# Attention pieces of the second half at doubled distances among the matrix products

## The chip, the cores and the metric

The kernel runs on one core of one Trainium2 chip. A core has five engines with queues of their own: TensorE (matrix products, written PE; its weight loads are written PEld), VectorE (DVE), ScalarE (ACT), GpSimd (POOL) and SyncE (SP), which here only issues transfers. Matrix products read SBUF and write PSUM, the accumulator memory; the weights come from HBM by DMA. The metric is the device time of one execution in microseconds. Three runs of the kernel before gave 2150.22, 2152.0 and 2154.43; the median is 2152.0.

## What is computed

A decoder trunk of two layers on 256 tokens of width 2048, all in float32. Cut to what matters:

```python
for l in range(2):
    h = rmsnorm(x)
    q, k, v, gate_b, gate_c, conv_in = split(h @ w_in[l])   # six parts of 1024 columns
    # 8 heads; each has two score maps m = 0, 1 of width 64
    s = einsum('bqhmd,bkhmd->bhmqk', q, k) * scale + bias   # causal
    p = softmax(s)
    p = p[:, :, 0] - lam * p[:, :, 1]                       # differential attention
    attn = rmsnorm(einsum('bhqk,bkhd->bqhd', p, v)) * (1 - lam_init)
    conv = gate_b * short_conv(gate_c * conv_in)            # 3 taps, causal
    x = x + concat([attn, conv]) @ w_out[l]
    x = x + square(relu(rmsnorm(x) @ w_up[l])) @ w_down[l]
```

## The kernel before, in words

Each layer is a *mixer* (attention and convolution, up to w_out) followed by an *mlp*. TensorE is meant to run matrix products without a break, and everything else is threaded between them. Every float32 product is made of three products of split operands: a weight tile `raw` is loaded by SP (L343), ACT copies its rounded high part to `whi` (L302), DVE subtracts to get the low part `wlo` (L303). `Weights.take` hands out such a pair and has the next three prepared. There are four `raw` buffers and three pairs, so the loads, ACT and DVE follow TensorE at a fixed distance.

The mixer makes its products in this order: q, k, v for heads 0 to 3; q, k, v for heads 4 to 7; then for each of four quarters of the convolution gc (gate_C) and ci (conv_in); then gb (gate_B) four times; then the output projection o. The gc, ci and gb products are made by `linear_t` (products at L408): each takes four weight tiles, and for each tile it issues eight products 512 wide with `whi` and eight 256 wide with `wlo`. After every four of these it calls `work.tick()`. One such tick is a *step*; a weight tile is four steps, a gc or ci product sixteen.

`work` is a list of background pieces, written as generators. `yield n` hands back and asks to go on n steps later; what is issued between two yields stands at that place in TensorE's program. TensorE's order is this order of tracing, kept as it is; the order on DVE, ACT, POOL and SP is chosen by a scheduler that simulates the times, so it follows from where the pieces are traced.

`attention(..., pace)` is such a piece, called once for heads 0 to 3 with pace 1 and once for heads 4 to 7 with pace 2. The second call begins 9 steps into the products gc. Each head is a generator `unit(i)` of three parts:

1. score: eight products into two PSUM banks (`sc`, L604); DVE adds the bias and takes the row maximum (L610), ACT the exponentials (L619), DVE the reciprocal sums and the difference of the two maps, into `s` (L622 to L630).
2. transpose: three transposes of `s` into a bank (`ptp`, L635); ACT and DVE make the high and low parts `pT` (L637, L638).
3. value: six products `av` (L646, L648); ACT and DVE add their parts into `ao` (L651, L652), and ACT sums the squares (L654).

The last head goes on with the norm: five small operations on POOL (L661 to L664), two multiplications `an` on DVE (L668), and, after a further distance, the transposes `atp` (L677) from which ACT and DVE write the output projection's operand `cat` (L681, L682). `staggered` starts the four heads a fixed number of steps apart and passes one step at a time.

Buffers that matter: three PSUM banks for `sc`, `ptp`, `atp` in turn, one bank for `av`, two buffers of `s`, one of `pT`, one of `ao`. The mlp's pool for the up weights (`uraw`, four buffers of 1 MB, loaded by SP at L809) lies in SBUF where the attention's bias, `s`, `pT` and `ao` were. So the first four loads of `uraw` can go out only when the attention is done with these; they stand in SP's queue among the loads of `raw`.

Of the kernel before, what the change touches and what calls it, by code (L numbers as in the profile page):

```python
# [88 lines left out]
def staggered(pieces, apart):  # L89

    entries = [[i * apart, p] for i, p in enumerate(pieces)]
    while entries:
        for e in list(entries):
            if e[0] <= 0:
                try:
                    e[0] = max(1, next(e[1]))
                except StopIteration:
                    entries.remove(e)
                    continue
            e[0] -= 1  # L100
        if entries:
            yield 1
# [3 lines left out]
def trunk(ctx: ExitStack, tc: tile.TileContext, x, w_in, w_out, conv_w, q_norm_g, k_norm_g,  # L106
# [19 lines left out]
    def bank(name):  # L126
        return ps.tile([P, CH], F32, tag="bank", name=name)
# [456 lines left out]
    def attention(l, qT, kT, kL, v, h0, dst, bias, tmp, pace):  # L584
# [9 lines left out]
        def unit(i):  # L594
# [31 lines left out]
            for t in range(NT):  # L626
# [2 lines left out]
                                               nlam[:, l:l + 1], op0=ALU.mult, op1=ALU.mult)  # L629
                nc.vector.scalar_tensor_tensor(p[:, w], s[:, 1, w], c[:, t:t + 1], s[:, 0, w],  # L630
                                               op0=ALU.mult, op1=ALU.add)
            yield 10
            tp = bank(f"ptp{h}")
            for b in range(3):
                nc.tensor.transpose(tp[:, b * P:(b + 1) * P], p[:, b * P:(b + 1) * P], ident)  # L635
            pT = tmp.tile([P, 2, 3 * P], F32R, tag="pT", name=f"pT{h}", bufs=1)
            nc.scalar.activation(pT[:, 0], tp[:, :3 * P], AF.Copy)  # L637
            nc.vector.tensor_sub(pT[:, 1], tp[:, :3 * P], pT[:, 0].bitcast(F32))  # L638
            yield 4

            av = ps.tile([P, CH], F32, tag="av", name=f"av{h}", bufs=1)
            av = av.rearrange("p (t n c) -> p t n c", t=NT, n=2)
# [23 lines left out]
            for t in range(NT):  # L666
# [3 lines left out]
                    ao[:, t].rearrange("p (g d) -> p g d", d=P),  # L670
                    f2[:, :, t:t + 1].to_broadcast([P, 4, P]), op=ALU.mult)
                an_.append(an)
            yield 12 if pace == 1 else 18
            for t in range(NT):
                tp = bank(f"atp{h0}_{t}")
                for b in range(4):
# [7 lines left out]
                    op0=ALU.mult, op1=ALU.subtract)  # L684
                yield 2

        yield from staggered([unit(i) for i in range(4)], 8)
        dst.ready = True

    def conv(l, q, u, cv, norm):  # L690
# [25 lines left out]
    def mixer(l, norm, loads):  # L716

        with ExitStack() as scope:
# [28 lines left out]
            for half in range(2):  # L747
                h0 = 4 * half
                acc = linear(f"q{l}{half}", hT, weights)
                r = norm.r  # L750
                qT = bpool.tile([P, 2, 4, S], F32R, tag="b", name=f"qT{l}{half}")
                work.start(qk_norm(acc, r, q_parts(qT), q_gain[:, l:l + 1], f"q{l}{half}"))
                acc = linear(f"k{l}{half}", hT, weights)
                kT = bpool.tile([P, 2, 4, S], F32R, tag="b", name=f"kT{l}{half}")
                work.start(qk_norm(acc, r, k_parts(kT, kL), k_gain[:, l:l + 1], f"k{l}{half}"))
                acc = linear(f"v{l}{half}", hT, weights)
                v = bpool.tile([P, 2, NT, CH], F32R, tag="b", name=f"v{l}{half}")
                for t in range(NT):
                    nc.scalar.activation(v[:, 0, t], acc[:, t], AF.Copy, scale=r[:, t:t + 1])
                    nc.vector.scalar_tensor_tensor(v[:, 1, t], acc[:, t], r[:, t:t + 1],  # L760
                                                   v[:, 0, t].bitcast(F32),
                                                   op0=ALU.mult, op1=ALU.subtract)
                work.start(attention(l, qT, kT, kL, v, h0, cat[half], bias, tmp,
                                     1 + half), 3 + 6 * half)
# [477 lines left out]
```

## Time and profile before

| what | value |
|---|---|
| median of three runs | 2152.0 |
| profiled execution | 2151.32 |
| span of its trace | 2149.5 |
| granted TensorE clock | 1.000 |
| PE busy | 2134.0 (99%) |
| PEld busy | 1819.9 (85%) |
| DVE busy | 1678.6 (78%) |
| ACT busy | 1308.2 (61%) |
| POOL busy | 169.8 (8%) |
| HBM traffic over the span | 221 GB/s |

The span is the time from the first to the last instruction; the profiled execution's own time is 1.8 longer. Busy times are sums over instructions. Matmuls are pipelined: one begins before the one ahead of it has ended, so lengths in a list of matmuls overlap, and what a piece costs is read from the distance between starts. A line of the timeline gives start, length, engine, source line, operation, output and inputs, tile and count; a bracket gives the idle time ahead of it and the instruction whose end released it. "whi" and "wlo" are the halves of a weight tile, "raw" is the tile as loaded.

### The profile page before, as it was taken

The numbers are of one execution on the slowest core, as the hardware profiler recorded it, in microseconds if no ns is written. First come the engines' busy times: TensorE is split into PE (matmuls) and PEld (weight loads), VectorE is DVE, ScalarE is ACT, GpSimd is POOL, SyncE is SP. The second block draws the span as 40 slices with busy tenths as digits, with TensorE's granted clock in tenths as the row PEclk, the third lists the DMA queues.
The fourth block names the chain that finished last, engine by engine and source line by source line (L and its number), as shares of the span: only waits on it lengthen the run. The fifth ranks groups of instructions, "written<-read, shape, count | busy, mean of one in ns | idle before, by whom it ended". The sixth has DMA issues, their size and how long they took to land. (4 is left out here: it accounts for less than half of the span.)

```text
span 2149.5 us, 28983 instructions
## 1 busy us (share of the span) xinstructions
PE 2134.0 (99%) x10934; PEld 1819.9 (85%) x10934; DVE 1678.6 (78%) x2297; ACT 1308.2 (61%) x1767; POOL 169.8 (8%) x226
## 2 busy tenths in 40 slices
PE   9999999999999999999999999999999999999999
PEld 8888888888888888888888888888888888888887
DVE  6777655799889888798566776557888888888984
ACT  6666445666666666565566654446666666665652
POOL 3111100000000000011110111000000000001110
PEclk9999999999999999999999999999999999999999
DMA  8555766577777777798665566656777777777984
GB/s 271 179 160 171 246 186 187 190 244 230 233 232 231 229 227 234 241 318 288 210 178 176 166 197 215 187 176 204 241 233 223 240 229 226 235 225 262 335 264 137
DMA packets 298524, 475.98 MB, mean 221 GB/s; under 512 B 10803, under 2 KB 191621, under 8 KB 298384
## 3 DMA queue, kind: packets, MB, share of 16 engines
q1 hardware_dynamic: 268768, 406.88, 60.4%
q0 software_dynamic: 29568, 67.24, 9.4%
q8 instruction: 85, 1.39, 0.3%
q14 instruction: 55, 0.45, 0.1%
q10 hardware_dynamic: 48, 0.02, 0.0%
HBM read 440.52 MB, written 33.58 MB: 221 GB/s over the span
## 5 line engine op out<-in xcount | busy, mean ns | idle before, releaser
L303 DVE TENSOR_TENSOR wlo<-raw,whi 128x1024 fp32r<-128x1024 f32 x286 | 352.2, 1234 | 252.3 <-ACT whi L302 245.8
L302 ACT ACTIVATE whi<-raw 128x1024 fp32r<-128x1024 f32 x286 | 303.1, 1060 | 341.1 <-PE o L386 73.6
L949 PE MATMUL upc<-nT,uhi 128*128 128x512 f32 x1920 | 477.7, 391 | 0.6 <-ACT ev L959 0.6
L816 ACT ACTIVATE uhi<-uraw 128x1024 fp32r<-128x1024 f32 x256 | 271.2, 1060 | 280.3 <-PE upc L949 260.4
L949 PEld LDWEIGHTS upc<-nT,uhi 128*128 128x128 f32 x1920 | 352.7, 188 | 69.2 <-ACT ev L959 1.1
L817 DVE TENSOR_TENSOR ulo<-uraw,uhi 128x1024 fp32r<-128x1024 f32 x256 | 312.9, 1223 | 109.3 <-ACT uhi L816 105.3
L949 PEld LDWEIGHTS upc<-nT,ulo 128*128 128x128 f32 x1920 | 261.9, 190 | 18.7
L949 PE MATMUL upc<-nT,ulo 128*128 128x256 f32 x1920 | 267.7, 282 | 0.0
L386 PE MATMUL o<-whi,cat 128*128 128x512 f32 x512 | 159.5, 390 | 0.0
L1074 PE MATMUL dn<-whi,fb 128*128 128x512 f32 x480 | 151.1, 389 | 0.0
L386 PEld LDWEIGHTS o<-whi,cat 128*128 128x128 f32 x512 | 96.1, 188 | 19.7
L302 ACT ACTIVATE whi<-uraw 128x1024 fp32r<-128x1024 f32 x60 | 63.7, 1061 | 75.7 <-PE dn L1074 70.7
L1074 PEld LDWEIGHTS dn<-whi,fb 128*128 128x128 f32 x480 | 90.1, 188 | 18.7
L386 PE MATMUL o<-wlo,cat 128*128 128x512 f32 x256 | 99.6, 389 | 0.0
L840 DVE TENSOR_TENSOR t13l<-t,t13h 128x1024 fp32r<-128x1024 f32 x78 | 95.5, 1224 | 4.0 <-ACT t13h L839 2.2
L839 ACT ACTIVATE b2h<-draw 128x1024 fp32r<-128x1024 f32 x78 | 82.5, 1058 | 24.9 <-PE pr L992 22.2
L840 DVE TENSOR_TENSOR b2l<-draw,b2h 128x1024 fp32r<-128x1024 f32 x78 | 95.5, 1224 | 2.1 <-ACT b2h L839 2.1
L840 DVE TENSOR_TENSOR t24l<-t,t24h 128x1024 fp32r<-128x1024 f32 x78 | 95.2, 1221 | 1.4 <-ACT t24h L839 0.3
L853 DVE TENSOR_TENSOR t<-draw 128x1024 f32<-128x1024 f32 x78 | 95.3, 1221 | 0.4
L992 PE MATMUL pr<-t13h,f 128*128 128x512 f32 x240 | 93.8, 391 | 0.0
L1074 PE MATMUL dn<-wlo,fb 128*128 128x512 f32 x240 | 93.4, 389 | 0.0
L303 DVE TENSOR_TENSOR wlo<-uraw,whi 128x1024 fp32r<-128x1024 f32 x60 | 73.2, 1224 | 21.1 <-ACT whi L302 20.9
(408 smaller groups left out, 4138.6 us busy)
## 6 DMA issues: line engine op xcount, KB each, us to landing
uraw<-in_w_up_dram SPq DMA_DIRECT2D x128, 1024.0 KB, 6.5
raw<-in_w_in_dram SPq DMA_DIRECT2D x191, 512.0 KB, 4.0
draw<-in_w_down_dram SPq DMA_DIRECT2D x82, 1024.0 KB, 5.3
raw<-in_w_out_dram SPq DMA_DIRECT2D x64, 512.0 KB, 3.6
uraw<-in_w_down_dram SPq DMA_DIRECT2D x30, 1024.0 KB, 6.3
raw<-in_w_down_dram SPq DMA_DIRECT2D x16, 1024.0 KB, 5.2
hid0p<-f POOLq DMA_DIRECT2D x21, 512.0 KB, 6.4
fb<-hid0p POOLq DMA_DIRECT2D x21, 512.0 KB, 5.9
```

What stands on the lines that cost most here:

```text
L302: pair = (nc.scalar.activation(hi, raw, AF.Copy), nc.vector.tensor_sub(lo, raw, hi.bitcast(F32)))
L303: nc.vector.tensor_sub(lo, raw, hi.bitcast(F32)))
L386: nc.tensor.matmul(acc[:, t], a.ap[:, pa, k % KG, t * P:(t + 1) * P], (hi, lo)[pw][:, j], start=(k == 0 and n == 0), stop=(k == nk - 1 and ...
L816: pair = (nc.scalar.activation(hi, src, AF.Copy), nc.vector.tensor_sub(lo, src, hi.bitcast(F32)))
L817: nc.vector.tensor_sub(lo, src, hi.bitcast(F32)))
L839: keep(nc.scalar.activation(hi, src, AF.Copy))
L840: keep(nc.vector.tensor_sub(lo, src, hi.bitcast(F32)))
L853: keep(nc.vector.tensor_sub(t[:, 0:2], raw[:, :, 1], raw[:, 0]))
L949: nc.tensor.matmul(acc[:, 0] if part else acc, wt[:, k], a.ap[:, 0, k % KG] if part else a.ap[:, :, k % KG], start=(part == 0 and kh == 0 ...
L992: nc.tensor.matmul(prods[n], f[:, pa, a], b[pw], start=(start and m == 0), stop=(stop and m == 2))
L1074: nc.tensor.matmul(prods[p], f[:, pa, 2 * k + t], b[pw][:, n], start=(p in starts and k == 0 and m == 0), stop=(stop and k == 1 and m == 2))
```

## The change

In the attention all distances are multiplied by `pace`. For heads 0 to 3 pace is 1 and nothing changes. For heads 4 to 7 pace is 2: score to transpose is 20 steps in place of 10, transpose to value 8 in place of 4, `an` to `atp` 24 in place of 18, and the heads start 16 steps apart in place of 8. The number of instructions on each engine is the same.

```diff
-            yield 10
+            yield 10 * pace
             tp = bank(f"ptp{h}")
...
-            yield 4
+            yield 4 * pace

             av = ps.tile([P, CH], F32, tag="av", name=f"av{h}", bufs=1)
...
-            yield 12 if pace == 1 else 18
+            yield 12 * pace
             for t in range(NT):
                 tp = bank(f"atp{h0}_{t}")
...
-        yield from staggered([unit(i) for i in range(4)], 8)
+        yield from staggered([unit(i) for i in range(4)], 8 * pace)
```

Where this puts the pieces (a product's tiles counted from 0):

| piece | before | after |
|---|---|---|
| score, heads 4 / 5 / 6 / 7 | gc0 tile 2 / ci0 tile 0 / ci0 tile 2 / gc1 tile 0 | gc0 tile 2 / ci0 tile 2 / gc1 tile 2 / ci1 tile 2 |
| transpose, heads 4 / 5 / 6 / 7 | ci0 tile 0 / ci0 tile 2 / gc1 tile 0 / gc1 tile 2 | ci0 tile 3 / gc1 tile 3 / ci1 tile 3 / gc2 tile 3 |
| value, heads 4 / 5 / 6 / 7 | ci0 tile 1 / ci0 tile 3 / gc1 tile 1 / gc1 tile 3 | gc1 tile 1 / ci1 tile 1 / gc2 tile 1 / ci2 tile 1 |
| `atp` | gc2 tile 0 | gc3 tile 3 |

Before, the transposes and values stand between a tile's narrow products; after, between its wide ones. In SP's queue the first loads of `uraw` stand behind 20 of the mixer's gc and ci weight loads before; after, three stand behind 30 of them and the fourth behind 31. On POOL the five operations of the norm stand behind the gc and cv multiplications (L769, L700) of the first quarter before; after, also behind both of the second quarter and the gc one of the third. In ACT's order before, the `pT` copy of a head stands ahead of the next head's exponentials; after, it stands behind them.

## The prediction

> **What bounds the kernel now.** I read the page's busy times first, then the stretch in which the change acts, then TensorE's waits there, then the order of TensorE's work at each wait. All times are microseconds.
>
> The page's first lines:
>
> ```profile
> span 2149.5 us, 28983 instructions
> PE 2134.0 (99%) x10934; PEld 1819.9 (85%) x10934; DVE 1678.6 (78%) x2297; ACT 1308.2 (61%) x1767; POOL 169.8 (8%) x226
> ```
>
> TensorE is busy for all but 15.5 of the span. So a change that neither adds nor removes matmuls can move the time only by how long TensorE stands, or by how well neighbouring matmuls overlap.
>
> The second half of the attention (heads 4 to 7) runs among the products gc, ci of the convolution. The busy times of each engine in the stretch from the first gc product to the first gb product, layer 0 and then layer 1 (columns: length, PE, PEld, DVE, ACT, POOL, granted clock, DMA share, GB/s):
>
> ```profile
> 156.18:259.05 102.87, 100.52 (x597) 88.26 (x596) 70.87 (x132) 59.39 (x112) 15.43 (x12) 1.00 0.64 205
> 1222.63:1326.82 104.19, 100.55 (x598) 88.27 (x597) 70.86 (x132) 59.39 (x112) 15.43 (x12) 1.00 0.64 202
> ```
>
> DVE is busy 69% of it and ACT 58%, the clock is 1.00: neither is the bound over the stretch, they are late only in places. The waits of TensorE between 155 and 260 (engine, line, who was waited for: total, times, longest):
>
> ```profile
> PE ptp L635 <- DVE s L630: 0.8, 1, 0.8
> PE sc L604 <- DVE cat L682: 0.6, 1, 0.6
> PE av L648 <- DVE pT L638: 0.5, 1, 0.5
> PE ci L408 <- ACT whi L302: 0.3, 1, 0.3
> ```
>
> Two of these are waits of a head on itself: the transposes ptp on the probabilities s, the products av on the low half of pT. The idle times understate them, because a matmul that restarts has lost its overlap with the one before; so I price each from start to start against the same work on time. First a product tile without pieces, then TensorE's order of layer 0 around the pieces (columns: start, length, line, operation, count; the bracket is idle time and who ended it):
>
> ```profile
> 250.67 2.00 PE L408 MATMUL ci<-nT,whi 128*128 128x512 f32 x8
> 252.51 1.11 PE L408 MATMUL ci<-nT,wlo 128*128 128x256 f32 x8
> 253.46 2.00 PE L408 MATMUL ci<-nT,whi 128*128 128x512 f32 x8
> ...
> 158.95 1.09 PE L408 MATMUL gc<-nT,whi 128*128 128x512 f32 x4
> 161.24 0.64 PE L408 MATMUL gc<-nT,wlo 128*128 128x256 f32 x4
> 162.63 1.09 PE L408 MATMUL gc<-nT,whi 128*128 128x512 f32 x4
> ...
> 172.72 0.64 PE L408 MATMUL ci<-nT,wlo 128*128 128x256 f32 x4
> 173.19 0.49 PE L635 MATMUL ptp<-ident,s 128*128 128x128 f32 x3
> 173.44 0.72 PE L408 MATMUL ci<-nT,wlo 128*128 128x256 f32 x4
> ...
> 175.84 0.64 PE L408 MATMUL ci<-nT,wlo 128*128 128x256 f32 x4
> 176.96 0.69 PE L408 MATMUL ci<-nT,wlo 128*128 128x256 f32 x4
> ...
> 183.37 0.63 PE L408 MATMUL ci<-nT,wlo 128*128 128x256 f32 x4
> 184.63 0.33 PE L648 MATMUL av<-v,pT 128*128 128x128 f32 x1 [0.51 <-DVE pT L638]
> 185.26 0.69 PE L408 MATMUL ci<-nT,wlo 128*128 128x256 f32 x4
> 186.71 0.39 PE L604 MATMUL sc<-kT,qT 128*128 128x128 f32 x2
> 188.54 0.64 PE L408 MATMUL gc<-nT,wlo 128*128 128x256 f32 x4
> 189.50 0.72 PE L408 MATMUL gc<-nT,wlo 128*128 128x256 f32 x4
> 191.90 0.64 PE L408 MATMUL gc<-nT,wlo 128*128 128x256 f32 x4
> 193.24 0.69 PE L408 MATMUL gc<-nT,wlo 128*128 128x256 f32 x4
> 195.61 0.63 PE L408 MATMUL gc<-nT,wlo 128*128 128x256 f32 x4
> 197.09 0.83 PE L635 MATMUL ptp<-ident,s 128*128 128x128 f32 x3 [0.85 <-DVE s L630]
> 197.68 0.71 PE L408 MATMUL gc<-nT,wlo 128*128 128x256 f32 x4
> ```
>
> A tile of products takes 253.46 − 250.67 = 2.79: 1.84 for the eight wide ones, 0.95 for the eight narrow ones. It is four steps, so a step is 0.70. A ptp on time makes half a tile's narrow products last 0.72 (172.72 to 173.44), an av 1.12 (175.84 to 176.96). Against these, layer 0 loses:
> - last ptp, 195.61 to 197.68: 2.07 − 0.72 = 1.35
> - the ptp before it, 188.54 to 189.50: 0.96 − 0.72 = 0.24
> - av at 183.37 to 185.26: 1.89 − 1.12 = 0.77
> - av at 191.90 to 193.24: 1.34 − 1.12 = 0.22
>
> That is 2.58. The fourth wait comes later, after the attention; here it is in both layers, with the transfer that makes it late:
>
> ```profile
> 223.98 1.11 PE L408 MATMUL gc<-nT,wlo 128*128 128x256 f32 x8
> 225.42 2.11 PE L408 MATMUL ci<-nT,whi 128*128 128x512 f32 x8 [0.33 <-ACT whi L302]
> ...
> 1290.46 1.11 PE L408 MATMUL gc<-nT,wlo 128*128 128x256 f32 x8
> 1293.18 2.12 PE L408 MATMUL ci<-nT,whi 128*128 128x512 f32 x8 [1.62 <-ACT whi L302]
> ```
>
> ```profile
> 207.54 6.60 SPq L809 DMA_DIRECT2D uraw<-in_w_up_dram  x4
> ```
>
> ```profile
> 224.31 1.06 ACT L302 ACTIVATE whi<-raw 128x1024 fp32r<-128x1024 f32 x1 [6.50 <-DMA raw<-in_w_in_dram]
> 225.66 1.06 ACT L302 ACTIVATE whi<-raw 128x1024 fp32r<-128x1024 f32 x1 [0.29 <-DMA raw<-in_w_in_dram]
> ```
>
> When the attention's buffers fall free, SP issues four loads of 1 MB for the next stage (uraw), and the 0.5 MB weight loads behind them arrive late: ACT stood 6.50 on one. TensorE lost 225.42 − 223.98 − 0.95 = 0.49 in layer 0, and 1293.18 − 1290.46 − 0.95 = 1.77 in layer 1. The two stretches above differ by 1.32, which is this wait's 1.28 and nothing else: so layer 1 has the same 2.58 of head waits.
>
> **The change part by part.** No instruction is added or removed on any engine; the compiled orders differ only in this stretch of each layer.
>
> Score to ptp goes from 10 to 20 steps: 14.0 and the pieces between. The slowest chain shown is head 7's, 186.71 to 197.09 = 10.4. The ptp waits (1.35 + 0.24 a layer) go, with at least 3.6 to spare. ptp to av goes from 4 to 8 steps, 5.6; the worst av was late by 0.77 at half that, so 2.0 to spare. The av waits (0.77 + 0.22) go. Heads stand 16 instead of 8 steps apart, so one head's chain no longer runs into the next one's.
>
> Where a piece stands: ptp and av move from between narrow products to between wide ones. Four transposes between wide ones cost 161.24 − 158.95 − 1.84 = 0.45, between narrow ones 162.63 − 161.24 − 0.95 = 0.44. So 0.01 a piece, up to 0.02, for 16 pieces over both layers: I take 0.2 as a cost. The ends are 0.2 of gain and 0.6 of loss.
>
> The first sc of head 4 keeps its place and its 0.6 wait on the buffer that the first half's cat frees. Nothing is counted.
>
> SP: the uraw loads move from behind 20 of the turned loads of weights (gc, ci) to behind 30 (three of them), then one weight load, then the fourth. The first weight load after the burst has 3 MB ahead of it, not 4. Late loads drain one 0.5 MB tile per 1.35 (224.31 to 225.66, both as soon as they landed), so 1 MB is 2.7. In place of 0.49 and 1.77 late it comes 2.2 and 0.9 early. The next one still has 4 MB ahead and lands 1.35 after the time of the present first, but is needed a tile, 2.79, later: 0.49 − 1.44 and 1.77 − 1.44, so early in layer 0 and 0.3 late in layer 1. Of the 2.26 of this wait I take 1.96 as gone; the ends are 0 (the burst costs the same again) and 2.26. The uraw loads themselves start ten tiles later, some 28; they are covered by the gb products and the whole output projection that follow; without that cover the first up products would be late by as much as the shift.
>
> POOL: the five small operations of the heads' norm move behind three more multiplications (gc twice, cv once); an, atp and the second cat come later. atp has 24 steps, 16.8, behind the last av in place of 18, and cat is read only by the output projection, after all gb products. No cost; if that cover went, the output projection would wait at its second act.
>
> DVE and ACT do the same work. In the new order ACT has the four exponentials of head 5 ahead of head 4's pT, and so on: a new coupling, priced below as the slower rival.
>
> Sum: 2 × 2.58 + 1.96 − 0.2 = 6.9 less. The profiled execution took 2151.3 (span 2149.5 and 1.8 around it), so 2144.4; the median of the runs is 0.7 above the profiled one, so **2145.1**.
>
> The Trainium skill, "DMA: Bandwidth & Descriptors", section "Queues, rings and completion order", says that each DMA engine takes the descriptors of one ring in ring order, which is what the step from 4 MB to 3 MB rests on; the landing of the late tiles one after another, 1.35 apart, agrees. Its section "Issuing engines are not separate DMA queues" says that transfers in flight interleave on the same 16 engines; if that held within SP's one queue too, the fourth load, issued right behind the weight load, would take back part of what it gave, and the time would be that of the second rival.
>
> **The rivals.**
> - All head waits go, the burst costs what it cost (0.49 and 1.77, only later, among the ci and gb products). For it: 4 MB still go out in one go, with the same need of weights beside them. Against: one weight load now goes ahead of the fourth. Gain 5.16 − 0.2 = 5.0: 2147.0.
> - The waits only change their place. For it: with TensorE no longer held up by ptp and av, the weights must come faster, and whi, wlo share ACT and DVE with the heads. Against: DVE at 69% and ACT at 58% of the stretch, with the heads' work now thinner. Gain 0 to 2: 2151.
> - Slower. ACT takes instructions in order, so head 4's pT stands behind head 5's exponentials, head 5's behind head 6's, head 6's behind head 7's; three av pieces a layer hang on it. The slowest exponentials in the trace ended 194.73 + 0.19 − 186.71 = 8.2 after that head's sc:
>
> ```profile
> 194.73 0.19 ACT L619 ACTIVATION_READ_ACCUMULATOR s<-s,nm 128x1 f32 x1
> ...
> L637 ACT ACTIVATE pT<-ptp x16: 467/472/492, 101.9 to 1264.5; 128x384 fp32r<-128x384 f32 x16
> L638 DVE TENSOR_TENSOR pT<-ptp,pT x16: 547/551/556, 102.6 to 1266.1; 128x384 fp32r<-128x384 f32 x16
> ```
>
>   With 0.47 and 0.55 for the two halves of pT that is 9.2; av of the head before stands 12 steps behind that sc, 8.4, and the pieces between (sc itself, a ptp). So it is about on time even at the slowest chain shown, which ran among three heads at once. It turns the sign if each of the six av pieces waits 1.2 (6.9 / 6), that is, if the chain takes over 10.5. At 2 each the time is 2145.1 + 12 = 2157.
>
> **How the numbers follow.** Forecast 0.62, same burst 0.14, waits moved 0.12, slower 0.12. Run to run the times spread from 2150.22 to 2154.43, so about 0.2%, 4.3, is what can be told from no change: the border is 2147.7. The first two cases lie under it (0.76, of which I give 0.01 to the middle), the third in it: faster 0.75, same 0.13, slower 0.12. The forecast's own range is 2143 to 2147: 7.4 gone without any cost, or 5, and 1 for the medians. The asked range goes up to the third case and leaves the slower one out: 2142.8 to 2151.
>
> **What the profile after would show.** TensorE's waits without ptp on s and without av on pT; sc on cat still at 0.6, twice. The stretch from the first gc to the first gb product 102.87 − 3.07 + 0.1 = 99.9 in layer 0 and 104.19 − 4.35 + 0.4 = 100.2 in layer 1, nothing else moved. The uraw loads behind the second of the four loads of the last ci product, and ci or gb waiting on whi there by 0.3 at most. The forecast is wrong if av waits on pT in several heads (the slower rival), if ci or gb waits on whi by over 1 in both layers (the burst), or if wlo, whi waits turn up between pieces (waits moved).

## The result, and the profile after

The changed kernel takes 2144.35 (median of five runs, 2142.89 to 2145.03); the ratio to the kernel before is 0.9963, with a 95% interval of 0.9952 to 0.9974. The profiled execution took 2144.35 as well, 6.97 less than the profiled execution before. The page of the kernel after begins:

```profile
span 2142.6 us, 28965 instructions
PE 2131.4 (99%) x10934; PEld 1818.4 (85%) x10934; DVE 1684.2 (79%) x2297; ACT 1308.7 (61%) x1767; POOL 165.4 (8%) x226
```

All waits of TensorE over the whole span after (engine, line, who was waited for: total, times, longest):

```profile
PE pr L992 <- DVE f L982: 3.2, 2, 1.7
PE sc L604 <- DVE cat L682: 1.2, 2, 0.6
PE warm L160 <- DVE mhalf L152: 1.1, 1, 1.1
PE upc L949 <- ACT ev L959: 0.5, 1, 0.5
PE ci L408 <- ACT whi L302: 0.4, 1, 0.4
```

ptp and av are gone from the list, in both layers. sc has kept its 0.6, and of the wait of ci on whi 0.4 is left. The busy times from the first gc to the first gb product after, layer 0 and layer 1 (the first number behind the stretch is its length):

```profile
155.66:255.45 99.79, 99.18 (x597) 87.80 (x596) 73.63 (x132) 59.43 (x113) 13.20 (x12) 1.00 0.64 204
1220.05:1320.50 100.45, 99.45 (x598) 87.86 (x597) 73.17 (x132) 58.75 (x111) 13.20 (x12) 1.00 0.64 200
```

The stretches are 3.08 and 3.74 shorter, 6.82 together: the whole gain but 0.15 lies where the change was made.

The last head's transpose and what is left of the load burst, in TensorE's order after (start, length; the bracket is the idle time and who ended it):

```profile
217.21 1.09 PE L408 MATMUL gc<-nT,whi 128*128 128x512 f32 x4
218.14 0.49 PE L635 MATMUL ptp<-ident,s 128*128 128x128 f32 x3
218.39 1.17 PE L408 MATMUL gc<-nT,whi 128*128 128x512 f32 x4
...
1316.10 1.11 PE L408 MATMUL ci<-nT,wlo 128*128 128x256 f32 x8
1317.60 2.11 PE L408 MATMUL ci<-nT,whi 128*128 128x512 f32 x8 [0.39 <-ACT whi L302]
```

The transposes follow 0.93 behind the four wide products and take 0.25, with no gap. ci waits only in layer 1, 1317.60 − 1316.10 − 0.95 = 0.55.

The burst of `uraw` loads, SP's issues and ACT's copies behind it, in layer 0 and layer 1 after:

```profile
232.51 3.84 SPq L809 DMA_DIRECT2D uraw<-in_w_up_dram  x3
236.44 3.21 SPq L343 DMA_DIRECT2D raw<-in_w_in_dram  x1
239.70 1.23 SPq L809 DMA_DIRECT2D uraw<-in_w_up_dram  x1
...
1296.91 3.83 SPq L809 DMA_DIRECT2D uraw<-in_w_up_dram  x3
```

```profile
246.47 1.06 ACT L302 ACTIVATE whi<-raw 128x1024 fp32r<-128x1024 f32 x1 [1.30 <-DMA raw<-in_w_in_dram]
250.61 1.06 ACT L302 ACTIVATE whi<-raw 128x1024 fp32r<-128x1024 f32 x1 [3.08 <-DMA raw<-in_w_in_dram]
...
1312.41 1.06 ACT L302 ACTIVATE whi<-raw 128x1024 fp32r<-128x1024 f32 x1 [2.84 <-DMA raw<-in_w_in_dram]
1316.49 1.06 ACT L302 ACTIVATE whi<-raw 128x1024 fp32r<-128x1024 f32 x1 [3.02 <-DMA raw<-in_w_in_dram]
```

In layer 0 the first weight tile behind three loads is used 246.47 − 232.51 = 14.0 after the burst began; before, behind four loads, it was 224.31 − 207.54 = 16.8. The second is used at 18.1, that is about 16.8 and one tile of 1.35. Over all the kernels below these times spread; the last section has them.

### The profile page after: what moved, and what is told of

Same layout as the page of the kernel before. It is cut to its first block, busy times and chain, and to the rows that moved or that the text cites. A ratio compares the mean times of both kernels' runs of the same rounds, so it can differ in the third digit from the quotient of the medians.

```text
span 2142.6 us, 28965 instructions
## 1 busy us (share of the span) xinstructions
PE 2131.4 (99%) x10934; PEld 1818.4 (85%) x10934; DVE 1684.2 (79%) x2297; ACT 1308.7 (61%) x1767; POOL 165.4 (8%) x226
## 4 chain that ended last, share of the span: by engine, by line
PE 96%; DMA 1%; DVE 1%; ACT 1%; issue 0%; SPq 0%; DVEq 0%; ACTq 0%
PE upc L949 30%; PE pr L992 13%; PE o L386 8%; PE dn L1074 8%; PE gb L408 4%; PE k L386 4%; PE v L386 4%; PE ci L408 4%; PE q L386 4%; PE gc L408 3%; PE dn L1143 3%; PE dn L992 2%; PE pr1r L992 1%; PE pr0r L992 1%; PE upw L949 1%; PE up L949 1%
## 5 line engine op out<-in xcount | busy, mean ns | idle before, releaser
L303 DVE TENSOR_TENSOR wlo<-raw,whi 128x1024 fp32r<-128x1024 f32 x286 | 356.9, 1249 | 235.3 <-ACT whi L302 233.8
```

Source lines behind the costliest of these rows:

```text
L303: nc.vector.tensor_sub(lo, raw, hi.bitcast(F32)))
```

## The experiments

The theory that the runs were to test is narrower than the prediction, which let the doubled distances and the wider spacing work together: the head waits come from *crowding*, heads whose chains run into each other on DVE and ACT, so the spacing between the heads pays. The rival is *distance*: a head's own 10 and 4 steps are too short. The load burst is a second cause of its own.

The kernel before was run again beside the experiments, and each ratio is to these runs: its median was 2151.3 beside the runs with the spacing alone, three loads, transpose to value at 4 steps and the changed kernel two steps later, and 2153.06 beside the other four. The intervals of most of the faster kernels overlap, so they are told apart by their waits and not by their times.

**The spacing alone**

```diff
-        yield from staggered([unit(i) for i in range(4)], 8)
+        yield from staggered([unit(i) for i in range(4)], 8 * pace)
```

> Heads 4 to 7 start 16 steps apart as after the change, but the distances inside a head are the old ones (10, 4, 18). Theory (crowding): the waits of ptp and av come from heads running into each other on DVE and ACT, not from the distances inside a head, since head 4, which has no head before it, was on time with 10 and 4 steps. Then all the 5.2 us of head waits go here too, the load burst costs what it costs after the change (0 to 0.5), and the time is 2144 to 2146. Rival (distance): 10 steps, some 7 us and the pieces, are too short for the chain of a head that took up to 10.4 us; the ptp and av waits stay, only the burst's 2 us go, and the time is 2149 to 2151.

Measured: 2146.1 (2144.26 to 2147.42), ratio 0.9973 [0.9963, 0.9983]. TensorE's waits in this kernel, those of the attention and the products:

```profile
PE gc L408 <- ACT whi L302: 2.3, 3, 1.1
PE sc L604 <- DVE cat L682: 1.2, 2, 0.6
```

No ptp and no av wait is left, with 10 and 4 steps inside a head. That is crowding. A head's chain, from its first sc to the end of the last operation on s (L630), shows it directly: for head 7 of layer 0 it ran from 186.71 to 197.43 before, 10.7, and takes 6.2 here. The last line of the chain before, then both ends of it here:

```profile
196.69 0.74 DVE L630 SCALAR_TENSOR_TENSOR s<-s,c 128x128 f32<-128x128 f32 x2
...
203.21 0.39 PE L604 MATMUL sc<-kT,qT 128*128 128x128 f32 x2
208.69 0.74 DVE L630 SCALAR_TENSOR_TENSOR s<-s,c 128x128 f32<-128x128 f32 x2
```

The time lies 0.1 above the theory's range, since the burst cost more than I gave it: gc waits on whi for 2.3 in three places, 1.06 in layer 0:

```profile
242.66 2.14 PE L408 MATMUL gc<-nT,whi 128*128 128x512 f32 x8 [1.06 <-ACT whi L302]
```

The attention ends earlier here, and the burst goes out at another place relative to the tiles. The two stretches from first gc to first gb take 101.09 and 101.52, together 2.37 longer than in the changed kernel, which is about this wait. So of the 6.82 that the change takes from them, the spacing alone takes 4.45.

**The distances alone**

```diff
-            yield 10
+            yield 10 if pace == 1 else 14
...
-            yield 4
+            yield 4 * pace
```

> The other part alone: heads 8 steps apart as before the change, but score to transpose 14 in place of 10 and transpose to value 8 in place of 4. Theory (crowding): longer distances without more room between the heads only make more heads live at once. With two buffers of s, head 6's first work on DVE must wait until head 4's value is squared, behind step 22, while its score stands at step 16; its two banks stay taken, and head 7's score at step 24 waits on them for 1 to 3 us in each layer. The waits of ptp and av go or shrink, that of sc comes: 2149 to 2156. Rival (distance): the ptp and av waits go as in the changed kernel and nothing comes: 2145 to 2148.

Measured: 2153.2 (2151.22 to 2155.47), ratio 1.0003 [0.9994, 1.0011]: no gain at all. Its waits:

```profile
PE ptp L635 <- DVE s L630: 3.1, 2, 1.6
PE sc L604 <- DVE mx L610: 1.9, 2, 1.0
PE sc L604 <- DVE pT L638: 1.9, 2, 1.0
PE sc L604 <- DVE cat L682: 1.2, 2, 0.6
```

av is gone, as expected, and sc waits on its banks twice a layer instead. The ptp wait did not shrink, it grew from 0.8 to 1.6 each. It is head 7's, and the trace lays it to the buffer of s: head 7's first sc is at 185.86, but DVE takes its maxima only at 195.63, after ACT has squared head 5's values and so given its buffer back:

```profile
194.44 0.30 ACT L654 ACTIVATE s<-ao 128x128 f32<-128x128 f32 x1
...
195.63 0.27 DVE L610 CUSTOM_DVE_ANT_0 s<-sc,bias 128x128 f32<-128x128 f32 x1
```

The chains of heads 6 and 7 take 15.4 and 15.5 here: a longer distance makes a head hold its buffer longer. The burst's wait was smaller (0.6 in all, in layer 1). So these longer distances alone change one wait for another, and the rival is refuted for them. They are not the change's in full: 14 steps stand for its 20, and `an` to `atp` stays at 18. With 20 and 8 at the old spacing head 4's value would stand at step 28, behind head 7's score at 24, which needs banks that are free only when head 6 has got head 4's buffer of s. By the order of the program that cannot go on; it was not run.

**Half of the spacing, distances as before**

```diff
-        yield from staggered([unit(i) for i in range(4)], 8)
+        yield from staggered([unit(i) for i in range(4)], 4 + 4 * pace)
```

> Half of the spacing: heads 12 apart, inner distances the old ones (10, 4, 18). Theory (crowding): a head's transpose at step 10 now stands ahead of the next head's score at 12, so its chain runs alone and the ptp waits (1.6 us a layer) go; its value at step 14 stands behind that score, so pT can still be late behind the next head's maxima on DVE: av waits of 0 to 0.8 us a layer. With the load burst's wait of 0 to 1.2 us a layer 2145 to 2149. Rival (distance): ptp and av wait as in the kernel before, and the time is 2149 to 2152.

Measured: 2147.96 (2145.61 to 2149.22), ratio 0.9975 [0.9966, 0.9985]. Neither ptp nor av is in the list of waits. What the products wait for is the burst, four loads in a row again in this kernel's queue:

```profile
PE ci L408 <- ACT whi L302: 2.6, 2, 1.8
```

From start to start one ptp is still late in each layer, head 6's, in layer 0 by 193.68 − 192.50 − 0.72 = 0.46; its idle times are too short for the list:

```profile
192.50 0.63 PE L408 MATMUL gc<-nT,wlo 128*128 128x256 f32 x4
193.18 0.74 PE L635 MATMUL ptp<-ident,s 128*128 128x128 f32 x3
```

This head's score stands in gc1 tile 0, where head 7's stood before, and there DVE and ACT also have the elementwise work of the first quarter of the convolution (L772, L694, L696). Its chain takes 9.0, those of heads 5 and 7 take 6.5 and 6.6. So a part of the lateness before belongs, it seems, to this place and not to the other heads; with the heads 12 apart the lateness at this place fell from 1.35 to 0.46. With heads 16 apart no score stands there.

**Half of the spacing with the doubled distances** (the changed kernel, edited)

```diff
-        yield from staggered([unit(i) for i in range(4)], 8 * pace)
+        yield from staggered([unit(i) for i in range(4)], 8 + 4 * (pace - 1))
```

> The changed kernel with its heads 12 in place of 16 apart (distances 20, 8, 24). Theory (crowding, with the buffers of s as its price): head 6's score stands at step 24, ahead of head 4's value at 28; its maxima wait on DVE for the buffer of s, and since the distances inside the head are long, TensorE still waits for none of it: no ptp or av wait, 2144 to 2147, what is over the changed kernel being the load burst. Rival (16 apart is needed): waits of 0.5 us or more on s, pT or a bank in each layer, 2147 to 2151.

Measured: 2146.72 (2143.91 to 2149.51), ratio 0.997 [0.996, 0.998]. No wait of ptp or av, and sc only at its old place:

```profile
PE gc L408 <- ACT whi L302: 3.4, 2, 2.0
PE sc L604 <- DVE cat L682: 1.2, 2, 0.6
```

The crowding theory again, with the price that it named: the chains of heads 6 and 7 take 13.7 and 12.8, and 20 steps are long enough for them. The 3.4 are the burst, here too with four loads in a row.

**The burst with three loads in place of four** (the kernel before, edited)

```diff
-            upool = scope.enter_context(tc.tile_pool(name="upool", bufs=4))
+            upool = scope.enter_context(tc.tile_pool(name="upool", bufs=3))
```

> The kernel before with three in place of four up-weight buffers, so that three 1 MB loads go out at once while the heads are as they were. Theory (the ci wait is the bandwidth that the burst takes, and loads of one queue land in their order): with 3 MB ahead in place of 4 the weight tile behind the burst lands 2.7 us earlier, so the wait of the products on whi behind the burst (0.49 us in layer 0, 1.77 in layer 1) is gone in both layers, and the head waits on s and pT stay. Rival (the wait has another cause, or the loads share the bandwidth so that the number ahead does not matter): TensorE still waits on whi for 0.3 to 1.8 us behind the burst. The whole time says nothing here, since the next stage has a buffer less; only the stretch from the first gc to the first gb product is read.

This is a single run. The waits within the attention's stretch are those of the heads alone, and the two layers are now equally long:

```profile
PE ptp L635 <- DVE s L630: 1.7, 2, 0.9
PE sc L604 <- DVE cat L682: 1.2, 2, 0.6
PE av L648 <- DVE pT L638: 1.0, 2, 0.5
```

```profile
156.05:258.36 102.31, 100.26 (x598) 88.20 (x597) 70.82 (x132) 59.55 (x112) 16.18 (x12) 1.00 0.62 196
1222.48:1324.78 102.30, 100.25 (x597) 88.19 (x596) 70.48 (x132) 59.54 (x112) 15.82 (x12) 1.00 0.62 196
```

102.87 − 102.31 = 0.56 and 104.19 − 102.30 = 1.89 went: the wait on whi in both layers, with the head waits as they were. The burst goes out earlier in this kernel (it needs less of the attention's space), so the run does not hold its place fixed, and by itself does not show that the number of loads is what counts. The first tile behind it is used 14.1 after the burst began in layer 0 and 13.8 in layer 1, against 14.0 and 15.5 in the changed kernel.

**Transpose to value at 4 steps** (the changed kernel, edited)

```diff
-            yield 4 * pace
+            yield 4
```

> The changed kernel with transpose to value at 4 steps again, everything else doubled. In ACT's order pT of a head stays behind the exponentials of the next one. Theory (the coupling named as the slower rival is real, and the 8 steps pay for it): av comes 8 steps and the pieces, some 6.9 us, behind the next head's sc, while the exponentials end some 6.5 to 8.2 us behind it and pT takes 1.0 more; heads 4, 5, 6 wait 0.7 to 1.5 us each in both layers, 4 to 9 us together, and the time is 2149 to 2153. Rival (the coupling is harmless): no av wait on pT of over 0.2 us, and the time is that of the changed kernel, 2144 to 2145.

Measured: 2143.53 (2142.68 to 2146.39), ratio 0.9966 [0.9952, 0.9979]. No av wait: the rival is right, and the coupling that the prediction named as the way to a slower kernel is harmless. ACT's and TensorE's lines for heads 5 and 4 show why:

```profile
180.93 0.19 ACT L619 ACTIVATION_READ_ACCUMULATOR s<-s,nm 128x1 f32 x1
181.02 0.47 ACT L637 ACTIVATE pT<-ptp 128x384 fp32r<-128x384 f32 x1
```

```profile
176.27 0.39 PE L604 MATMUL sc<-kT,qT 128*128 128x128 f32 x2
183.12 0.28 PE L646 MATMUL av<-v,pT 128*128 128x256 f32 x1
```

pT of head 4 does stand behind the exponentials of head 5. But these end 181.12 − 176.27 = 4.9 behind that head's first sc, not 8.2; the 8.2 were those of a crowded head.

**The second half two steps later** (the changed kernel, edited)

```diff
                 work.start(attention(l, qT, kT, kL, v, h0, cat[half], bias, tmp,
-                                     1 + half), 3 + 6 * half)
+                                     1 + half), 3 + 8 * half)
```

> The changed kernel with its second half traced two steps later (a start distance of 11 in place of 9). Theory: the one wait that the change left, head 4's sc on the bank that cat frees (0.6 us idle, 0.7 from start to start, in each layer), is late by less than the two steps, 1.4 us; it goes, and all pieces stand between narrow products again at the same price; the time is 1.4 lower than that of the changed kernel, 2142.5 to 2143.5. Rival (where a piece stands has a price that the wait hid, or the wait moves with it): 2144 or more, with the sc wait still there or the stretch from first gc to first gb not shorter.

Measured: 2141.86 (2141.24 to 2142.34), ratio 0.9956 [0.9943, 0.9968], the lowest time of all. All its waits:

```profile
PE pr L992 <- DVE f L982: 3.3, 2, 1.6
PE warm L160 <- DVE mhalf L152: 1.1, 1, 1.1
PE q L386 <- DVE wlo L303: 0.2, 1, 0.2
```

```profile
155.71:254.55 98.84, 98.84 (x598) 88.00 (x596) 70.62 (x132) 58.85 (x112) 14.57 (x12) 1.00 0.65 205
1218.65:1317.49 98.84, 98.84 (x598) 88.00 (x596) 70.66 (x132) 58.88 (x112) 14.57 (x12) 1.00 0.64 205
```

The sc wait is gone and so is the burst's; in both stretches TensorE is busy all the time. 99.79 − 98.84 = 0.95 in layer 0 is the sc wait, 0.83 as priced in the last section, and 0.1 left over, which may be what standing between the wide products costs. The time is 0.6 below the theory's range: the burst's 0.55 of layer 1, which the theory had not counted, went too. Against 98.84 the kernel before lost 4.03 in layer 0, of which the head waits, the burst and the sc wait are 2.58 + 0.49 + 0.83 = 3.90.

**The second half two steps later in the kernel before**

```diff
-                                     1 + half), 3 + 6 * half)
+                                     1 + half), 3 + 8 * half)
```

> The kernel before with its second half traced two steps later, which stands its pieces in the other half of the tiles. Theory: the wait of head 4's score on the bank goes as it did in the changed kernel so started (0.7 us a layer), the crowding of the heads and the ptp and av waits of 2.6 us a layer stay: 1 to 3 us under the kernel before, 2148 to 2151. Rival (what decides is where the pieces stand within a tile, not how far apart the heads are): the ptp and av waits go with it, 2144 to 2146.

Measured: 2146.43 (2144.93 to 2147.01), ratio 0.9968 [0.9956, 0.9981]: 6.6 under the kernel before where the theory gave 1 to 3, and just over the rival's range. Its waits on heads and weights:

```profile
PE ptp L635 <- DVE s L630: 1.6, 4, 0.6
PE ci L408 <- ACT whi L302: 0.2, 1, 0.2
```

ptp still waits, in four places, as the theory has it: from start to start 0.40 and 1.13 in layer 0, 1.53 against the 1.35 + 0.24 before. But the av waits went with the shift, as the rival has it, and the scheduler split the burst into three and one here too, so that 1.7 of its wait went. So where the pieces stand is enough to remove the av and sc waits, while the ptp wait fell only in the runs with wider spacing; neither of the two pictures holds alone. With the heads still 8 apart this shift gains nearly as much as the change (ratios 0.9968 and 0.9963).

**How long a head's chain is.** First sc to the end of s, layer 0; layer 1 is the same within 0.2:

| kernel | heads 4 / 5 / 6 / 7 |
|---|---|
| before | 7.1 / 7.9 / 10.8 / 10.7 |
| after | 7.1 / 6.6 / 6.7 / 6.7 |
| spacing alone | 7.1 / 6.2 / 6.2 / 6.2 |
| distances alone | 7.1 / 7.7 / 15.4 / 15.5 |
| 12 apart | 7.1 / 6.5 / 9.0 / 6.6 |
| 12 apart, doubled distances | 7.1 / 6.2 / 13.7 / 12.8 |
| before, two steps later | 9.2 / 8.7 / 8.5 / 10.1 |

The heads meet not only on DVE and ACT but at the two buffers of s. In the kernel before, head 6's maxima begin 4.5 behind its first sc (182.92 − 178.41), head 5's 1.4; head 4's squares, which free the buffer, end at 182.1. In the kernel before two steps later the bracket of head 6's maxima names it:

```profile
180.98 0.29 DVE L610 CUSTOM_DVE_ANT_0 s<-sc,bias 128x128 f32<-128x128 f32 x1 [0.71 <-ACT s L654]
```

How much of the crowding is the buffers and how much the engines is open: a third buffer of s at the old spacing was not tried.

## Why the prediction was right

The time forecast was 2145.1, and for the profiled execution 2144.4; they came out at 2144.35 both, since the median was not 0.7 above the profiled execution this time. The steps:

- *The ptp and av waits go*, 2.58 a layer. They did. Layer 0 became 3.08 shorter, against 3.07 − 0.1 forecast; layer 1 3.74, against 4.35 − 0.4. The pricing from start to start held: the idle times in the list of waits gave only 1.3 a layer. Its reason, lost overlap, covers only a part of what the idle times leave out (see the last section).
- *Why they go* was argued wrongly in one point. The prediction held the doubled distances, 14.0 against a chain of 10.4 and 5.6 against 4, for what removes the waits, and the spacing only for a help. The runs show the reverse: the spacing alone removes them all at 16 steps and all but 0.46 a layer at 12, and longer distances alone (14 and 8) give nothing. The 10.4 was not what a head needs, but what it needs among others and beside the convolution's own work; with the heads 16 apart it is 6.2. The change contains both parts, so this error did not touch the time: the sum was right with a cause half wrong.
- *Where a piece stands*, 0.2 of cost. Without its late pieces the layer 0 stretch before would be 102.87 − 2.58 − 0.56 less the sc wait, the one after 99.79 less the same wait: 99.73 against 99.79: 0.06 in layer 0, where 0.1 was taken (the 0.56 is the burst's wait as the run with three loads gave it; with the prediction's 0.49 nothing is left). The shifted kernel above gave 0.1 by another way. So the cost is at most the one taken.
- *The sc wait stays*, 0.6 twice: it did.
- *The burst.* Forecast for the first tile behind it: 2.7 earlier than behind four loads. Measured 16.8 − 14.0 = 2.8 in layer 0; in layer 1 it was used 1312.41 − 1296.91 = 15.5 after the burst began, 2.6 earlier than the 18.1 before. Forecast for the next tile: on time in layer 0, 0.3 late in layer 1. Measured: on time, and 0.39 idle or 0.55 from start to start. That it came out so closely owes something to luck: the same order of loads left 1.06 and 1.27 of idle time in the kernel with the spacing alone, where the burst falls elsewhere among the tiles.
- *The order in the queue.* That the first tile gained about a whole load's time speaks for the ring order of the Trainium skill's "DMA: Bandwidth & Descriptors", section "Queues, rings and completion order". It speaks against the rival that the burst costs the same again, the first of the prediction's list, which the prediction itself calls the second. Whether the fourth load takes a part back from the weight load ahead of it is not told: the first tile was used after 14.1 and 13.8 with no fourth load, and after 14.0 to 15.8 with one.
- *POOL, the later atp and the later uraw loads* cost nothing: none of their readers is in the list of waits. The burst in layer 0 went out 25.0 later than before, where some 28 was forecast.
- *The slower rival* was built on a chain of 8.2 taken from a crowded head. With the heads apart it is 4.9, so the case had less in it than the 0.12 that it got.

## What to carry to other kernels

When a wait repeats in a pipelined piece of work, find out whether the piece is too slow for its distance or whether copies of it meet on the same engine or buffer: here the same 10 steps were enough with copies 16 apart, nearly enough with copies 12 apart and too few with copies 8 apart, and longer distances at the old spacing only moved the wait to the buffers. Try the place as well: two steps later, with nothing spread out, gained nearly as much as the change. A burst of prefetches in the queue of the loads that the busy engine lives on has a price that depends on what stands between its parts and where it falls among the tiles: three big loads, an urgent one and the fourth left waits of 0 to 1.3 a layer, four in a row 0.3 to 2.0. Price a wait from start to start against the same piece on time, not by its idle time.

## What had not been expected of the hardware

A matrix product that comes late costs more than the engine's idle time. Idle times of 0.33 and 1.62 before a ci product cost 0.49 and 1.77, some 0.16 more each: a narrow product lasts until 0.16 after the place where the next one would begin on time (1.11 against 0.95), and this overlap is lost. 0.60 before a score cost 0.83 (its place between wide products took 1.75 and 0.92 on time, in the lines of the kernel after that follow). The 0.85 before a transpose that cost 1.35 is more than lost overlap. The bracket there gives only the first wait: the second transpose begins at 197.48, just behind the second operation on s, which ends at 197.43.

```profile
163.04 0.22 PE L604 MATMUL sc<-kT,qT 128*128 128x128 f32 x1
164.79 1.07 PE L408 MATMUL gc<-nT,whi 128*128 128x512 f32 x4
...
175.96 0.39 PE L604 MATMUL sc<-kT,qT 128*128 128x128 f32 x2
176.88 1.07 PE L408 MATMUL ci<-nT,whi 128*128 128x512 f32 x4
```

And the same burst does not always take the same time. From its start to the use of the first tile behind it, four loads took 16.8 and 18.1 before (layers 0 and 1), 18.2 and 17.2 with heads 12 apart, 18.4 and 17.9 with these and the doubled distances. Three loads took 13.8 to 15.8 over all kernels, 14.0 and 15.5 in the changed one. The two groups do not meet, so the number of loads ahead counts; the spread of up to 2 within a group is as large as the waits that are at stake, and neither layer is always the slower. What makes it so no run here tells; it stays open.
